# Tokens kept by remainder by four in a hybrid decoder block, and the first head group's values projected per slot

## The chip, the cores and the metric

The kernel runs on one core of one Trainium2 chip. The metric is the device time of one execution in microseconds, taken as the median of several runs. A profile is one more execution, recorded by the hardware profiler, with a time of its own.

## The reference

One layer on 512 tokens of width 1024, all in float32: a half-step SwiGLU network, then a mixing stage of a convolution branch and an attention branch, a second half-step network, a gated per-layer input and a final norm.

```python
h = h + 0.5 * swiglu(rms_norm(h, g_ffn1), ...)          # 1024 -> 2816 -> 1024
u = rms_norm(h, g_mix)
a_glu, q, k, v, gate_logits = split(u @ w_in)
y_conv = conformer_conv(a_glu, ...)                      # GLU, causal depthwise conv of 31, layer norm, swish, matmul
q, k = rotary(q), rotary(k)                              # 12 heads of 128: 3 groups x 4 slots
for (window, dilation) in ((128, 1), (512, 4), (2048, 16)):      # one group each
    o_g, lse_g = dilated_window_attention(q, k, v, dilation, window // dilation)
alpha = softmax over the 3 groups of lse
o = sum_g alpha_g * o_g                                  # per slot; 4 slots x 128
h = h + (sigmoid(gA) * y_conv + sigmoid(gB) * (o @ w_attn_out)) @ w_mix_out
h = h + 0.5 * swiglu(rms_norm(h, g_ffn2), ...)
h = h + sigmoid(rms_norm(h, g_ple) @ w_ple_gate) * (p @ w_ple_proj)
return rms_norm(h, g_final)
```

A query of group 0 sees the 128 tokens before it. In groups 1 and 2 a query sees only tokens at distances that are multiples of 4 (or of 16), so attention there stays within a class of tokens with the same remainder by four.

## The kernel before

Activations are held transposed: a tile has 128 channels on the partitions and the 512 tokens along the free dimension, so 1024 channels are 8 tiles (`KD`). To keep float32 precision each operand is split into a high and a low float32r half, and each product is three matmuls (`mm3`: high by high, high by low, low by high). A `unit` (8 k-steps of `mm3`, 24 matmuls of 512 columns) projects 128 output channels for all tokens.

Weights come in slabs of 128 x 1024, in a fixed list (`slab_order`). `slab(key)` takes the next one and issues the loads of later ones: raw loads six slabs ahead, the remainder for the low half (an ACT copy at L296 and an accumulating DMA at L298) up to four ahead. The POOL queue loads the keys in `POOLED`, SP the others; keys in `RAISED`, such as `v0`, go through one more buffer. Slabs, their halves and two score tiles (`sc`) per slot share 16 buffers (`NW`).

The program is written out in the order in which each engine runs it; nothing is reordered. Work that can wait, above all the convolution's taps on VectorE (L819), lies in the list `bg`; `background(n)` takes n entries from it at places fixed by the constants `N_GLU`, `N_QK`, `N_V0`, `N_V` and `N_GATE`. `soon` holds exponentials and scalings of attention, `between` the subtractions of turned scores, `lns` the layer norm's steps.

The stages around the change:

1. First network. Its last round of `down` adds each of 8 output tiles to the residual h (L703); `into` splits it for the next stage.
2. GLU: 16 units (a gate half and a value half per 128 channels), each product scaled by the inverse norm R, and the taps of the convolution start in `bg`.
3. First values (L1069 to L1080): the values of group 0 for all four slots, 96 matmuls with 128 tokens as the stationary operand and 512 weights moving. The result has tokens on the partitions. The norm factor per token is needed as a column: `rcol` by blocks of 128 tokens, and `rcls` by class, brought by two DMAs through DRAM (`exchange`).
4. Four slots. In each: six units for q and k of the three groups, each followed by `rotary`; then the values of groups 1 and 2 (L1102 to L1111), whose stationary operand is a class of tokens. For slots 1 to 3 and the gates after them, attention of the slot before (`before`) is woven in: `last` makes the scores of groups 1 and 2, `weigh` combines the groups, `turn` transposes the weighted scores, `values` multiplies them. Since the groups' statistics lie by block and by class, `exchange` carries them through DRAM (L885, L886) from one order to the other.
5. 16 units of merge gates with the rest of the convolution, then the attention projection (`pb`), the convolution's (`py`) and the mix (`px`), and the second network.

PSUM has six banks for all of this and two for the convolution's accumulators.

Tokens lie in their natural order. Where an operation needs a class, it reads every fourth token:

```python
def by_class(t):  return t.rearrange("p (i c) -> p c i", c=NB)      # a strided view
def classes(t):   return t.rearrange("p (c i) -> p c i", c=NB)      # 4 contiguous parts
xh, xl = (by_class(z)[:, c] for z in us[4 * j + kk])                # L1107
```

Of the kernel before, what the change touches and what calls it, by code (L numbers as in the profile page):

```python
# [18 lines left out]
P = 128  # L19
# [6 lines left out]
HD = 128  # L26
# [50 lines left out]
N_QK = ((2, 0, 1),) * 2 + ((1, 0, 0),) + ((2, 0, 1),) + ((1, 0, 1),) * 2  # L77
N_V0, N_V = 1, 1
# [52 lines left out]
def block_kernel(ctx: ExitStack, tc: tile.TileContext, a, out):  # L131
# [18 lines left out]

    def bank(n="ps", tag="ps"):
        return psum.tile([P, S], F32, name=name(n), tag=tag, bufs=6 if tag == "ps" else 2)
# [28 lines left out]
    def sources(key):  # L181

        if key[0] == "v0":
            return [(slice(0, 2), slice(i * HD, (i + 1) * HD), blocks_of(a["w_v"][i, key[1]], 2)[:, :, :HD])
                    for i in range(NSLOT)]
# [130 lines left out]
    def split_one():  # L316
        i = state["split"]
        if i in halves:
            state["split"] = i + 1
            return  # L320
        r, q, kind = raws.pop(i), product(order[i]), order[i][0]
        if q is not None:
            w = r.shape[-1]
            h, l = W("wh", F32R)[:, :w], W("wl", F32R)[:, :w]
            spend(0.25 + w * 0.00075, 0.17 + w * 0.001)
            A.activation(h, r, AF.Copy)  # L326
            V.tensor_sub(l, r, h.bitcast(F32))  # L327
            halves[i] = h, l
        elif kind == "pg":
            hs, ls, low = [], [], W("wl", F32R)  # L330
            for c in range(2):
                z = r[:, c * S:(c + 1) * S]
                h, l = T("pgh", F32R), low[:, c * S:(c + 1) * S]
                A.activation(h, z, AF.Copy)
                V.tensor_sub(l, z, h.bitcast(F32))
                hs.append(h)
                ls.append(l)
            halves[i] = (hs, ls)
        else:
            w = r.shape[-1]  # L340
            h, l = W("wh", F32R)[:, :w], W("wl", F32R)[:, :w]
            A.activation(h, r, AF.Copy)
            V.tensor_sub(l, r, h.bitcast(F32))
            halves[i] = (h, l)
        state["split"] = i + 1
# [194 lines left out]
    def ffn(n, xs, norm, resid, after):  # L540
        lo, hi = slice(0, 256), slice(256, 512)
        hid = []
        xn = [None] * 4
# [142 lines left out]
        def down(r, first_, end):  # L686
            ks = ROUNDS[r]
            for m in range(first_, end):
# [14 lines left out]
                V.scalar_tensor_tensor(resid[m], p, 0.5, resid[m], op0=OP.mult, op1=OP.add)  # L703
# [40 lines left out]
    def tables():  # L744
# [19 lines left out]
        do(V.tensor_copy, ang, ip)  # L764
# [38 lines left out]
    for at, w, c in ((0, 2 * P, C_M[0]), (2 * P, P, P), (3 * P, P, C_M[2] - P)):  # L803
        nc.sync.dma_start(mask[:, at:at + w], a["cst"][:, c:c + w])
    conv = {}
    summed = []

    def conv_start(cs, glus):
# [7 lines left out]
        for s in range(1, TAPS):  # L816
            for c, g, acc in zip(cs, glus, accs):
# [4 lines left out]
        def end(c, acc):  # L822
            t = T("cv")
            A.activation(t, acc, AF.Copy)
            conv[c] = t
            if not summed:
                summed.append(T("csum"))
                V.tensor_copy(summed[0], acc)
            else:
                V.tensor_add(summed[0], summed[0], acc)  # L830
        for c, acc in zip(cs, accs):
            bg.append(lambda c=c, acc=acc: end(c, acc))

# [3 lines left out]
    def glu(c, p1, p2, tg, g_, halves_=(0, 1)):  # L837
# [4 lines left out]
        if 1 in halves_:  # L842
            V.tensor_mul(g_, p2, R[0])
            V.tensor_mul(g_, g_, tg)
# [23 lines left out]
    R, rcol = R[0], rcols[0]  # L868
    z = None

    def by_class(t):

        return t.rearrange("p (i c) -> p c i", c=NB)

    def classes(t):
        return t.rearrange("p (c i) -> p c i", c=NB)

    def exchange(what, w, by_block, by_cls):

        for i, (src, dst) in enumerate((by_block, by_cls)):  # L880
# [3 lines left out]
            blk, cls = t.rearrange("(b p) e -> p b e", p=P), t.rearrange("(i c) e -> i c e", c=NB)  # L884
            nc.sync.dma_start((blk, cls)[i], src)  # L885
            nc.sync.dma_start(dst, (cls, blk)[i])  # L886

    rcls = const.tile([P, NB], F32, name="rcls")
    exchange("r", 1, (rcol.rearrange("p (b e) -> p b e", e=1), rcls.rearrange("p (b e) -> p b e", e=1)), (None, None))
# [9 lines left out]
    def rotary(p, n, extra, cls, fill=(lambda: None,) * 2):  # L899
# [14 lines left out]
        if cls:  # L914
            t, hh, ll = by_class(t), classes(h), classes(l)
# [9 lines left out]
    class Attention:  # L925
# [3 lines left out]
        def __init__(self, slot, q, k):  # L929
            self.slot, self.q, self.k = slot, q, k  # L930
# [9 lines left out]
        def score(self, x):  # L940
            p = bank("sc")
            t, lo = self.place(x)
            b = x % NB
            c = slice(b * P, (b + 1) * P)
            if x < NB:
                q, k = self.q[0], self.k[0]
                mm3(p[:, lo:2 * P], q[0][:, c], q[1][:, c], *(z[:, (b - 1) * P + lo:(b + 1) * P] for z in k), True, True)
            else:
                for g in (1, 2):
                    q, k = self.q[g], self.k[g]  # L950
                    mm3(p[:, (g - 1) * P:g * P], q[0][:, c], q[1][:, c], k[0][:, c], k[1][:, c], g == 1, g == 2, True)
            m0 = x // NB * 2 * P
            V.tensor_tensor_reduce(out=t, in0=p[:, lo:2 * P], in1=mask[:, m0 + lo:m0 + 2 * P], op0=OP.add, op1=OP.max,
                                   scale=1.0, scalar=-3.0e38, accum_out=self.own_[:, x, 0:1])

        def scores(self, xs):
            return {i + 4: lambda x=x: self.score(x) for i, x in enumerate(xs)}
# [66 lines left out]
        def values(self, i):  # L1024
# [3 lines left out]
            for j in range(2):  # L1028
                if i < 2:
                    kb = 2 * i + j  # L1030
                    w = P if kb == NB - 1 else 2 * P
                    vh, vl = v0[kb]
                    c, z = slice(self.slot * HD, (self.slot + 1) * HD), slice(j * 2 * P, j * 2 * P + w)
# [8 lines left out]
            if i == 1:  # L1042
                self.first = self.po
            if i == 3:
                t = T("ot")
                A.activation(t.rearrange("p (i c) -> p c i", c=NB), classes(self.po), AF.Copy)
                V.tensor_add(t, t, self.first)
# [20 lines left out]

    pv = [bank("pv") for _ in range(NB)]  # L1069
    for j in range(4):  # L1070
        wh, wl = (blocks_of(z, 2) for z in slab(("v0", j)))
        for b in range(NB):
            for kk in range(2):
                xh, xl = (z[:, b * P:(b + 1) * P] for z in us[2 * j + kk])
                PE.matmul(pv[b], xh, wh[:, kk], start=j == 0 and kk == 0, stop=False)
                PE.matmul(pv[b], xh, wl[:, kk], start=False, stop=False)
                PE.matmul(pv[b], xl, wh[:, kk], start=False, stop=j == 3 and kk == 1)
            background(N_V0)
    v0 = [split(pv[b], "v", rcol[:, b:b + 1]) for b in range(NB)]
    pv = None  # L1080

    before = None
    for s in range(NSLOT):
        q, k = [], []
        n = 0
        now = Attention(s, q, k)
        for g in range(NG):
            for base, dst in ((16, q), (28, k)):
                p = bank("pq")
                unit(p, ("win", base + 4 * g + s), us,  # L1090
                     beside=before.last() if n == 0 and before else now.scores(range(NB)) if n == 3 else {})
                if before is not None:
                    before.step(n)
                if n == 3:
                    now.soft(range(NB))
                dst.append(rotary(p, "qk", N_QK[n], g > 0, *([before.fill(n)] if before else [])))
# [3 lines left out]
                n += 1  # L1100
        q = k = None
        pv = [bank("pv") for _ in range(2)]  # L1102
        for j in range(2):
            wh, wl = (blocks_of(z, 4) for z in slab(("v", s, j)))
            for kk in range(4):
                for c in range(NB):
                    xh, xl = (by_class(z)[:, c] for z in us[4 * j + kk])  # L1107
# [4 lines left out]
                if at == 2 and before is not None:  # L1112
                    before.step(6)
                    before = None
# [191 lines left out]
    def put_out(b):  # L1306
        y = sums.pop(b)
        for i, (t, c, w) in enumerate(done.pop(b)):
# [4 lines left out]
            nc.sync.dma_start(out[b * P:(b + 1) * P, c:c + w], t)  # L1313
# [90 lines left out]
```

## Time and profile before

| | us |
|---|---|
| median of 3 runs (lowest, highest) | 1350.1 (1349.81, 1350.49) |
| the profiled execution | 1348.61 |
| its span | 1346.8 |
| TensorE busy | 1329.9 |
| VectorE busy | 837.3 |
| ScalarE busy | 693.4 |

Lines of the profile's groups read: line, engine, operation, output <- inputs, shape, count, then busy us in all and mean ns of one, then idle time of the engine just before and what ended it. PE is a TensorE matmul, PEld a weight load (it overlaps matmuls), DVE VectorE, ACT ScalarE. Lines of the order of time begin with start and duration in us. Lines of stages read: stretch, its length, busy us (and count) of PE, PEld, DVE, ACT and POOL, the granted TensorE clock, the DMA share and GB/s. Lines of waits read: engine, output, line, `<-` what it waited for, us in all, times, longest. Durations of matmuls overlap; starts do not.

### The profile page before, as it was taken

Reading aid. Unit: us, or ns where it says so; the run is one execution under the profiler, and the core shown is the slowest. Engines: PE = TensorE matmul, PEld = TensorE weight load, DVE = VectorE, ACT = ScalarE, POOL = GpSimd, SP = SyncE. Lnnn points to the kernel's source line nnn. Section 1 sums busy time; section 2 is a strip of 40 time slices with the busy share of each in tenths; the row PEclk is TensorE's granted clock in tenths of the full one; section 3 lists DMA queues with packets and bytes.
Section 4 is the critical chain, followed back from the end, with each engine's and each line's share of the span. In section 5 each row is a group of like instructions: output and inputs, shape, how many; then the busy total and the mean of one; then the engine's idle time right before and its main releaser. Section 6 shows DMA issues by size and latency. Waiting matters only on the chain.

```text
span 1346.8 us, 19358 instructions
## 1 busy us (share of the span) xinstructions
PE 1329.9 (99%) x7490; PEld 1182.7 (88%) x7490; DVE 837.3 (62%) x1371; ACT 693.4 (51%) x981; POOL 225.4 (17%) x294
## 2 busy tenths in 40 slices
PE   9999999999999999999999999999999999999997
PEld 7899899898888889899998888788899899998886
DVE  6985576442469775757665877656784357362465
ACT  6666367464433353636364534334477356555552
POOL 2112011112221231312121220002111111112100
PEclk9999999999999999999999999999999999999999
DMA  9579677878989775848474785233668866869641
GB/s 290 136 168 235 172 157 181 225 168 193 221 196 211 177 154 128 156 102 165 102 166 104 178 205 140 81 105 100 144 167 198 203 174 161 204 159 224 165 94 63
DMA packets 102419, 221.24 MB, mean 164 GB/s; under 512 B 16312, under 2 KB 38200, under 8 KB 102328
## 3 DMA queue, kind: packets, MB, share of 16 engines
q0 software_dynamic: 45856, 133.19, 48.6%
q1 hardware_dynamic: 56184, 86.56, 20.1%
q8 instruction: 59, 0.97, 0.3%
q14 instruction: 32, 0.26, 0.1%
q10 hardware_dynamic: 288, 0.26, 0.1%
HBM read 164.37 MB, written 2.14 MB: 124 GB/s over the span
## 4 chain that ended last, share of the span: by engine, by line
PE 94%; DVE 3%; issue 1%; ACT 1%; DMA 1%; ACTq 0%; SPq 0%; DVEq 0%; POOLq 0%
PE pd L367 8%; PE pd L368 8%; PE pd L369 8%; PE pa L367 6%; PE pa L368 6%; PE pa L369 6%; PE pq L367 3%; PE pq L368 3%; PE pq L369 3%; PE pg L367 3%; PE pg L368 3%; PE pg L369 3%; PE pv L1109 2%; PE pv L1111 2%; PE pv L1110 2%; PE pb L367 1%
## 5 line engine op out<-in xcount | busy, mean ns | idle before, releaser
L298 POOL DMA_DIRECT2D wl<-wr x106 | 91.7, 865 | 528.4 <-ACT wl L296 481.3
L819 DVE SCALAR_TENSOR_TENSOR acc<-glu,taps,acc 128x511 f32<-128x511 f32 (+14 forms) x240 | 161.1, 733 | 0.0
L296 ACT ACTIVATE wl<-wr 128x1024 fp32r<-128x1024 f32 (+1 forms) x106 | 108.1, 1020 | 78.1 <-DMA wl<-wr 34.0
L367 PE MATMUL pd<-hidh,wh 128*128 128x512 f32 x352 | 137.0, 389 | 0.0
L368 PE MATMUL pd<-hidl,wh 128*128 128x512 f32 x352 | 137.0, 389 | 0.0
L369 PE MATMUL pd<-hidh,wl 128*128 128x512 f32 x352 | 136.9, 389 | 0.0
L367 PE MATMUL pa<-bh,wh 128*128 128x256 f32 x432 | 122.5, 283 | 1.6 <-ACT p L666 1.6
L369 PE MATMUL pa<-bh,wl 128*128 128x256 f32 x432 | 122.4, 283 | 0.6 <-DVE wl L327 0.6
L310 ACT ACTIVATE wh<-wr 128x1024 fp32r<-128x1024 f32 (+1 forms) x106 | 107.6, 1015 | 29.8 <-DMA wl<-wr 26.3
L368 PE MATMUL pa<-bl,wh 128*128 128x256 f32 x432 | 122.2, 283 | 0.0
L327 DVE TENSOR_TENSOR wl<-s,wh 128x1024 fp32r<-128x1024 f32 x54 | 66.0, 1223 | 69.5 <-ACT wh L326 69.4
L296 ACT ACTIVATE wl<-wh 128x1024 fp32r<-128x1024 f32 x76 | 79.6, 1050 | 49.1 <-DMA wh<-in_w_in 25.6
L298 POOL DMA_DIRECT2D wl<-in_w_in x56 | 47.9, 855 | 293.6 <-ACT wl L296 279.4
L367 PEld LDWEIGHTS pa<-bh,wh 128*128 128x128 f32 x432 | 82.9, 192 | 2.0 <-ACT p L666 2.0
L369 PEld LDWEIGHTS pa<-bh,wl 128*128 128x128 f32 x432 | 82.9, 192 | 0.8 <-DVE wl L327 0.8
L368 PEld LDWEIGHTS pa<-bl,wh 128*128 128x128 f32 x432 | 82.9, 192 | 0.0
L703 DVE SCALAR_TENSOR_TENSOR gx<-pd,gx 128x512 f32<-128x512 f32 x48 | 32.9, 689 | 79.9 <-PE pd L369 79.9
L367 PE MATMUL pd<-bh,wh 128*128 128x256 f32 x288 | 82.0, 285 | 0.5 <-ACT p L666 0.4
L368 PE MATMUL pd<-bl,wh 128*128 128x256 f32 x288 | 81.5, 283 | 0.0
L369 PE MATMUL pd<-bh,wl 128*128 128x256 f32 x288 | 81.5, 283 | 0.0
L369 PEld LDWEIGHTS pd<-hidh,wl 128*128 128x128 f32 x352 | 66.1, 188 | 13.9
L367 PEld LDWEIGHTS pd<-hidh,wh 128*128 128x128 f32 x352 | 66.1, 188 | 13.5
(293 smaller groups left out, 3767.7 us busy)
## 6 DMA issues: line engine op xcount, KB each, us to landing
wl<-wr POOLq DMA_DIRECT2D x90, 512.0 KB, 5.6
wh<-in_w_in POOLq DMA_DIRECT2D x56, 512.0 KB, 7.1
wl<-in_w_in POOLq DMA_DIRECT2D x56, 512.0 KB, 5.7
wr<-in_w_ffn_up SPq DMA_DIRECT2D x80, 256.0 KB, 4.3
wr<-in_w_ffn_gate SPq DMA_DIRECT2D x78, 256.0 KB, 5.0
wr<-in_w_ffn_down SPq DMA_DIRECT2D x32, 512.0 KB, 5.7
wr<-in_w_ffn_down SPq DMA_DIRECT2D x16, 384.0 KB, 8.3
wl<-wr POOLq DMA_DIRECT2D x16, 384.0 KB, 5.4
```

The costliest lines, as they stand in the source:

```text
L296: A.activation(l.bitcast(F32R), h, AF.Copy, scale=-1.0)
L298: G.dma_start(to, src, accum_op=OP.add)
L310: A.activation(h, r, AF.Copy)
L327: V.tensor_sub(l, r, h.bitcast(F32))
L367: PE.matmul(ps, wh, xh, start=start, stop=False, skip_group_check=part)
L368: PE.matmul(ps, wh, xl, start=False, stop=False, skip_group_check=part)
L369: PE.matmul(ps, wl, xh, start=False, stop=stop, skip_group_check=part)
L703: V.scalar_tensor_tensor(resid[m], p, 0.5, resid[m], op0=OP.mult, op1=OP.add)
L819: bg.append(lambda acc=acc, g=g, w=w, s=s: V.scalar_tensor_tensor(acc[:, s:], g[:, :S - s], w, acc[:, s:], op0=OP.mult, op1=OP.add))
L1109: PE.matmul(po, xh, wh[:, kk], start=at == 0 and c % 2 == 0, stop=False, skip_group_check=True)
L1110: PE.matmul(po, xh, wl[:, kk], start=False, stop=False, skip_group_check=True)
L1111: PE.matmul(po, xl, wh[:, kk], start=False, stop=at == KD - 1, skip_group_check=True)
```

## The change

From the end of the first network on, tokens are kept by class: position c*128 + i holds token 4i + c. The last round of the first network writes h in that order, and the positions, the GLU's output, the convolution's, the mask of group 0 and p are brought into it or out of it where they are made; the convolution itself still runs in natural order. The output rows are written with a step of four. A class is then contiguous. Group 0, which works on blocks of 128 neighbouring tokens, finds its block in four runs of 32 (`by_block`), so its q, k, values and the norm factor for them are read by blocks, and within a block the tokens lie by class too.

The first values' stage goes. Each slot begins with a unit that projects its group 0 values as it does a query (weights stationary, 512 tokens moving), multiplies by R, and transposes the result in four 128 x 128 pieces beside the next unit (`turn0`, at the fifth k-step). `rcls` comes directly from the norm, without DRAM. Two scores share a PSUM bank. An exchange of statistics takes five DMAs instead of two. The sums over the convolution's channels are made from the copies in SBUF.

```diff
-N_QK = ((2, 0, 1),) * 2 + ((1, 0, 0),) + ((2, 0, 1),) + ((1, 0, 1),) * 2
-N_V0, N_V = 1, 1
+N_QK = ((2, 0, 1),) * 6
+N_V0, N_V = 4, 1
+N_TURN = 4
...
-    out += [("v0", j) for j in range(4)]
     for s in range(NSLOT):
+        out += [("v0", s)]
...
+    def by_block(t):
+        return t.rearrange("p (c b i) -> p b c i", c=NB, b=NB)
+    def blocks(t):
+        return t.rearrange("p (b c i) -> p b c i", c=NB, b=NB)
...
-                V.scalar_tensor_tensor(resid[m], p, 0.5, resid[m], op0=OP.mult, op1=OP.add)
+                if n == "1" and r == len(ROUNDS) - 1:
+                    old, resid[m] = resid[m], spare[0]
+                    V.scalar_tensor_tensor(classes(resid[m]), by_class(p), 0.5, by_class(old), op0=OP.mult, op1=OP.add)
+                    spare[0] = old
...
-            V.tensor_mul(g_, p2, R[0])
-            V.tensor_mul(g_, g_, tg)
+            V.tensor_mul(p2, p2, R[0])
+            V.tensor_mul(by_class(g_), classes(p2), classes(tg))
...
-            A.activation(t, acc, AF.Copy)
+            A.activation(classes(t), by_class(acc), AF.Copy)
...
-    R, rcol = R[0], rcols[0]
+    R, rcls = R[0], rcols[0]
...
-            blk, cls = t.rearrange("(b p) e -> p b e", p=P), t.rearrange("(i c) e -> i c e", c=NB)
-            nc.sync.dma_start((blk, cls)[i], src)
-            nc.sync.dma_start(dst, (cls, blk)[i])
-    rcls = const.tile([P, NB], F32, name="rcls")
-    exchange("r", 1, ...)
+            cls = t.rearrange("(c i) e -> i c e", c=NB)
+            blk = t.rearrange("(c b i) e -> c i b e", c=NB, b=NB)
+            if i:
+                nc.sync.dma_start(cls, src)
+            for c in range(NB):
+                z = slice(c * P // NB, (c + 1) * P // NB)
+                if i:
+                    nc.sync.dma_start(dst[z], blk[c])
+                else:
+                    nc.sync.dma_start(blk[c], src[z])
+            if not i:
+                nc.sync.dma_start(dst, cls)
...
-        if cls:
-            t, hh, ll = by_class(t), classes(h), classes(l)
+        if blk:
+            t, hh, ll = by_block(t), blocks(h), blocks(l)
...
             if i == 1:
-                self.first = self.po
+                self.first = T("ot")
+                A.activation(by_block(self.first), blocks(self.po), AF.Copy)
             if i == 3:
-                t = T("ot")
-                A.activation(t.rearrange("p (i c) -> p c i", c=NB), classes(self.po), AF.Copy)
-                V.tensor_add(t, t, self.first)
+                t = self.first
+                V.tensor_add(t, t, self.po)
...
-    pv = [bank("pv") for _ in range(NB)]
-    for j in range(4):
-        wh, wl = (blocks_of(z, 2) for z in slab(("v0", j)))
...
-    v0 = [split(pv[b], "v", rcol[:, b:b + 1]) for b in range(NB)]
...
+        p = bank("pq")
+        unit(p, ("v0", s), us, beside=before.last() if before else {})
+        v0 = T("v0")
+        V.tensor_mul(blocks(v0), by_block(p), by_block(R))
+        if before is not None:
+            before.step(0)
+        some(6)
+        background(N_V0)
+        def turn0():
+            p = bank("pt")
+            for b in range(NB):
+                PE.transpose(p[:, b * P:(b + 1) * P], v0[:, b * P:(b + 1) * P], ident)
+            now.v0 = split(p, "v")
...
                 unit(p, ("win", base + 4 * g + s), us,
-                     beside=before.last() if n == 0 and before else now.scores(range(NB)) if n == 3 else {})
+                     beside=now.scores(range(NB)) if n == 4 else {N_TURN: turn0} if n == 1 else {})
...
-                    xh, xl = (by_class(z)[:, c] for z in us[4 * j + kk])
+                    xh, xl = (classes(z)[:, c] for z in us[4 * j + kk])
...
-                if at == 2 and before is not None:
-                    before.step(6)
...
-            nc.sync.dma_start(out[b * P:(b + 1) * P, c:c + w], t)
+            nc.sync.dma_start(out.rearrange("(i c) e -> c i e", c=NB)[b][:, c:c + w], t)
```

In the new loop n counts from 1 after the values' unit, so `step`, `fill` and `late` act one unit of q or k earlier than before; `step(6)` now follows the sixth q or k unit.

More of the change, by code (lines that the diff above doesn't have):

```diff
@@ L149, in T, with by_class, classes @@
         return act.tile([P, w], dt, name=name(n), tag="t", bufs=NT)
+    def by_class(t):
+        return t.rearrange("p (i c) -> p c i", c=NB)
+    def classes(t):
+        return t.rearrange("p (c i) -> p c i", c=NB)
+    def by_block(t):
+        return t.rearrange("p (c b i) -> p b c i", c=NB, b=NB)
+    def blocks(t):
+        return t.rearrange("p (b c i) -> p b c i", c=NB, b=NB)
     def bank(n="ps", tag="ps"):
@@ L542, in ffn @@
         hid = []
+        spare = []
         xn = [None] * 4
@@ L762, in reduce @@
                 less(t, n, w)
-        do(V.tensor_copy, ang, ip)
+        do(V.tensor_copy, classes(ang), by_class(ip))
         do(V.tensor_scalar, ang, ang, freq, None, op0=OP.mult)
@@ L802, in block_kernel @@
     mask = T("mask")
-    for at, w, c in ((0, 2 * P, C_M[0]), (2 * P, P, P), (3 * P, P, C_M[2] - P)):
+    for at, w, c in ((2 * P, P, P), (3 * P, P, C_M[2] - P)):
         nc.sync.dma_start(mask[:, at:at + w], a["cst"][:, c:c + w])
+    window = T("window")[:, :2 * P]
+    for c in range(NB):
+        nc.sync.dma_start(window[c * P // NB:(c + 1) * P // NB, :],
+                          a["cst"].rearrange("(i c) k -> c i k", c=NB)[c][:, C_M[0]:C_M[0] + 2 * P])
+    bg.append(lambda: V.tensor_copy(mask[:, :2 * P].rearrange("p (z c i) -> p z c i", z=2, c=NB),
+                                    window.rearrange("p (z i c) -> p z c i", z=2, c=NB)))
     conv = {}
@@ L816, in conv_start @@
         for s in range(1, TAPS):
+            if s == 3 and cs[0]:
+                bg.append(lambda: sum_up((cs[0] - 2, cs[0] - 1)))
             for c, g, acc in zip(cs, glus, accs):
@@ L823, in end, with sum_up @@
             t = T("cv")
-            A.activation(t, acc, AF.Copy)
+            A.activation(classes(t), by_class(acc), AF.Copy)
             conv[c] = t
[L826 to L830, printed above, removed]
         for c, acc in zip(cs, accs):
             bg.append(lambda c=c, acc=acc: end(c, acc))
+        if cs[1] == KD - 1:
+            bg.append(lambda: sum_up(cs))
+    def sum_up(cs):
+        if not summed:
+            summed.append(T("csum"))
+            V.tensor_add(summed[0], *(conv[c] for c in cs))
+        else:
+            for c in cs:
+                V.tensor_add(summed[0], summed[0], conv[c])
     R, glus, rcols = [], [], []
@@ L867, in block_kernel, with exchange @@
             glus = []
-    R, rcol = R[0], rcols[0]
+    R, rcls = R[0], rcols[0]
     z = None
[L871 to L880, printed above, removed]
+    def exchange(what, w, by_blk, by_cls):
+        for i, (src, dst) in enumerate((by_blk, by_cls)):
             if src is None:
@@ L938, in place, with score @@
             return self.sc[x // NB][:, x % NB * 2 * P + lo:(x % NB + 1) * 2 * P], lo
[L940 to L954, printed above, removed]
+        def score(self, xs):
+            bank_ = bank("sc")
+            ps = [bank_[:, i * 2 * P:(i + 1) * 2 * P] for i in range(2)]
+            for x, p in zip(xs, ps):
+                b = x % NB
+                c = slice(b * P, (b + 1) * P)
+                if x < NB:
+                    lo, q, k = self.place(x)[1], self.q[0], self.k[0]
+                    mm3(p[:, lo:], q[0][:, c], q[1][:, c], *(z[:, (b - 1) * P + lo:(b + 1) * P] for z in k), True, True)
+                else:
+                    for g in (1, 2):
+                        q, k = self.q[g], self.k[g]
+                        mm3(p[:, (g - 1) * P:g * P], q[0][:, c], q[1][:, c], k[0][:, c], k[1][:, c], g == 1, g == 2, True)
+            for x, p in zip(xs, ps):
+                t, lo = self.place(x)
+                m0 = x // NB * 2 * P
+                V.tensor_tensor_reduce(out=t, in0=p[:, lo:], in1=mask[:, m0 + lo:m0 + 2 * P], op0=OP.add, op1=OP.max,
+                                       scale=1.0, scalar=-3.0e38, accum_out=self.own_[:, x, 0:1])
         def scores(self, xs):
-            return {i + 4: lambda x=x: self.score(x) for i, x in enumerate(xs)}
+            return {i + 4: lambda x=x: self.score((x, x + 1)) for i, x in enumerate(xs) if i % 2 == 0}
         def last(self):
@@ L1084, in block_kernel @@
         q, k = [], []
-        n = 0
-        now = Attention(s, q, k)
+        now = Attention(q, k)
+        p = bank("pq")
+        unit(p, ("v0", s), us, beside=before.last() if before else {})
+        v0 = T("v0")
+        V.tensor_mul(blocks(v0), by_block(p), by_block(R))
+        p = None
+        if before is not None:
[7 more added lines that the diff above has]
+            now.v0 = split(p, "v")
+        n = 1
         for g in range(NG):
@@ L1090, in block_kernel @@
                 unit(p, ("win", base + 4 * g + s), us,
-                     beside=before.last() if n == 0 and before else now.scores(range(NB)) if n == 3 else {})
+                     beside=now.scores(range(NB)) if n == 4 else {N_TURN: turn0} if n == 1 else {})
                 if before is not None:
                     before.step(n)
-                if n == 3:
+                if n == 4:
                     now.soft(range(NB))
-                dst.append(rotary(p, "qk", N_QK[n], g > 0, *([before.fill(n)] if before else [])))
+                dst.append(rotary(p, "qk", N_QK[n - 1], g == 0, *([before.fill(n)] if before else [])))
                 p = None
```

35 lines of the change are left out of this document (17 added, 18 removed).

## The prediction

> **What bounds the kernel now.** I read the page first, then what TensorE waits for, then its groups by form.
>
> ```profile
> span 1346.8 us, 19358 instructions
> PE 1329.9 (99%) x7490; PEld 1182.7 (88%) x7490; DVE 837.3 (62%) x1371; ACT 693.4 (51%) x981; POOL 225.4 (17%) x294
> PE 94%; DVE 3%; issue 1%; ACT 1%; DMA 1%; ACTq 0%; SPq 0%; DVEq 0%; POOLq 0%
> PE py L368 <- DVE cvl L385: 2.4, 2, 1.3
> ```
>
> TensorE is busy for all but 16.9 us, and the last line heads the list of what it waits for: 2.4 us in all, in 2 times. (Its granted clock is the 1.00 in the stage rows below.) So time can come only from fewer or faster TensorE instructions, and time is lost only where the others newly let it wait. VectorE (62%) and ScalarE (51%) have room on average. The next question is whether every matmul runs as fast as its shape allows.
>
> ```profile
> L1109 PE MATMUL pv<-wh,xsh 128*128 128x256 f32 x128 | 50.9, 397 | 0.0
> L367 PE MATMUL pa<-bh,wh 128*128 128x256 f32 x432 | 122.5, 283 | 1.6 <-ACT p L666 1.6
> L1109 PEld LDWEIGHTS pv<-wh,xsh 128*128 128x128 f32 x128 | 42.0, 328 | 0.0
> L367 PEld LDWEIGHTS pa<-bh,wh 128*128 128x128 f32 x432 | 82.9, 192 | 2.0 <-ACT p L666 2.0
> L1075 PEld LDWEIGHTS pv<-wh,xsh 128*128 128x128 f32 x32 | 6.0, 188 | 1.3
> 563.92 0.40 PE L1109 MATMUL pv<-wh,xsh 128*128 128x256 f32 x1
> ...
> 571.38 0.40 PE L1111 MATMUL pv<-wh,xsl 128*128 128x256 f32 x1
> ```
>
> ```profile
> 235.28 0.28 PE L369 MATMUL pd<-bh,wl 128*128 128x256 f32 x1
> ...
> 237.08 0.28 PE L369 MATMUL pd<-bh,wl 128*128 128x256 f32 x1
> ```
>
> They do not. The values of groups 1 and 2 (L1109 to L1111, three lines of 128) have 256 moving columns, as the mixed products of the networks have. Durations overlap, so I take starts: from 563.92 to 571.38 there are 32 steps, 0.233 us each; from 235.28 to 237.08 there are 15, 0.120 us each. The same 256 columns cost nearly double. What differs is the weight load: 328 ns against 192. Its source is `by_class(z)[:, c]`, every fourth token, 16 bytes apart; L1075 loads from the same tiles, contiguous, in 188. This part is bound by the strided load.
>
> **The change, part by part.**
>
> *The strided load goes.* With tokens kept by remainder, `classes(z)[:, c]` is 128 neighbours. 96 matmuls per slot in 4 slots, 384 x (0.233 - 0.120) = 43.4 us, all of it on TensorE and so on the path. Bounds: no gain, if the layout is not what sets the 0.233 (a rival below), and 46.8 if it fell to the 0.111 of a 128-column step (the row of transposes below shows 0.90 us for 8). I take 0.120, the row with the same columns.
>
> The Trainium skill, "SBUF — State Buffer" (the cacheline note under "Door 1: The DMA port swizzle"), states 16-byte lines, with a penalty where each access crosses to a new one; fp32 at a step of four is that case, and the 328 against 188 ns agrees.
>
> *The first group's values.* Before, 96 matmuls of 512 columns in a stage of their own; after, 24 per slot, still 512 columns, weights and tokens changing places. Same number, same pace: 0. New are four transposes per slot.
>
> ```profile
> 562.48 0.90 PE pt L1016 x8
> 444.90:466.80 21.90, 21.90 (x98) 18.16 (x97) 17.63 (x27) 5.63 (x7) 5.85 (x9) 1.00 0.95 207
> 523.60:588.70 65.10, 65.10 (x329) 59.22 (x328) 43.38 (x84) 34.58 (x64) 15.29 (x20) 1.00 0.63 130
> ```
>
> 16 x 0.90/8 = +1.8 us. They come after four k-steps, 12 matmuls of 21.90/98 = 0.22 us, 2.7 us after the unit's end, and need only VectorE's product with R, at most 1.1 us by the strided rows below. Pairing scores changes neither their number nor columns: 0.
>
> *VectorE in a slot.* The second row above is slot 1: 65.1 us, VectorE 43.4. After: 65.1 + 5.4 (24 x 0.223) + 0.5 (transposes) - 10.9 = 60.1 us. VectorE gains 8 convolution taps (N_QK sums to 18 against 14, N_V0 gives 4), the product with R and the low half of the turned values, and loses strided reads.
>
> ```profile
> L819 DVE SCALAR_TENSOR_TENSOR acc<-glu,taps,acc 128x511 f32<-128x511 f32 (+14 forms) x240 | 161.1, 733 | 0.0
> 541.22 0.69 DVE L920 TENSOR_TENSOR qkl<-rot,qkh 128x512 fp32r<-128x512 f32 x1
> 554.21 1.11 DVE L920 TENSOR_TENSOR qkl<-rot,qkh 128x512 fp32r<-128x512 f32 x1 [0.55 <-ACT qkh L916]
> L1046 ACT ACTIVATE ot<-po 128x512 f32<-128x512 f32 x4 | 4.3, 1084 | 14.6 <-PE po L369 14.6
> ```
>
> L920 takes 0.69 on a contiguous `rot` (group 0) and 1.11 by class. Four of six per slot were strided; after, only group 0's two are, by blocks, in runs of 32. No row shows runs of 32, so between 0.69 and 1.11. Sum: 43.4 + 8 x 0.73 + 1.1 + 0.7 - 4 x 0.42 + (0 to 0.8) = 49.3 to 50.1 of 60.1 us. It stays under TensorE by 10 us, which is the cover for all of this. If the cover fails in a single unit, the units behind it (5.4 us each) absorb it, since PSUM has six banks.
>
> *Strided writes and reads elsewhere.* The first network's last round writes h by class (8 operations), the GLU writes by class (8), ScalarE copies 8 convolutions by class, and the positions, the window mask and pT once each. Each is priced between 0 and +0.42 us on VectorE, with two strided inputs perhaps double; on ScalarE less than the 1.08 us that its whole strided copy (L1046) takes. The tightest places:
>
> ```profile
> 403.00:414.00 11.00, 11.00 (x50) 9.12 (x49) 9.96 (x16) 2.65 (x3) 1.41 (x2) 1.00 1.05 267
> 356.81 0.69 DVE L703 SCALAR_TENSOR_TENSOR gx<-pd,gx 128x512 f32<-128x512 f32 x1 [1.25 <-PE pd L369]
> 358.29 0.75 DVE L388 SCALAR_TENSOR_TENSOR xsl<-gx,xsh 128x512 fp32r<-128x512 f32 x1 [0.79 <-ACT xsh L387]
> ```
>
> In the GLU, VectorE is busy 9.96 of 11.0 us; +0.42 per pair of units fits. At the end of the first network the chain after the last matmul is 356.81 to 359.04, 2.2 us; the next unit's eighth k-step comes 21 x 0.22 = 4.7 us after it, so +0.8 is hidden. Where ScalarE empties an accumulator, the next pair's first tap waits up to two such copies, 2.2 us, but the two sums that stood there (1.5 us by the row below) move behind it. Cost: 0.
>
> *The end of the convolution.* 128 list entries are spent in the slots against 112 before (with the first values' stage), so 60 entries remain for the gates against 72 (four entries of sums are added, the 12 GLU calls take 72 in both): 10 gate units instead of 12.
>
> ```profile
> 795.87 1.48 DVE L830 TENSOR_TENSOR csum<-csum,acc 128x512 f32<-128x512 f32 x2
> 834.54 2.47 DVE cv L1144 x4
> 843.59 0.50 PE py L368
> ```
>
> The sums now end about 796, VectorE's normalizing runs until `py` starts, and that is the 2.4 us wait quoted first. Two gate units (four steps of the list `lns`) earlier, it ends inside the attention projection. -2.4 us, bounds 0 and -2.4.
>
> *DMAs and queues.* SP no longer moves R through DRAM. It carries four loads for each first-values slab, now amid the slots, and five transfers instead of two per exchange of statistics, 0.33 us of issue each.
>
> ```profile
> 601.77 0.33 SPq L885 DMA_DIRECT2D st<-own  x1
> 603.18 0.37 SPq L886 DMA_DIRECT2D other<-st  x1
> 625.04 0.37 SPq L885 DMA_DIRECT2D st<-own  x1
> 633.86 0.33 SPq L886 DMA_DIRECT2D other<-st  x1
> other<-st SPq DMA_DIRECT2D x8, 4.0 KB, 3.4
> ```
>
> ```profile
> 607.59 0.69 DVE L901 TENSOR_TENSOR rot<-pq,nl 128x512 f32<-128x512 f32 x1 [0.68 <-PE pq L369]
> 608.20 0.16 DVE L987 TENSOR_TENSOR jm<-own,other 128x8 f32<-128x8 f32 x1
> 612.23 1.10 DVE L920 TENSOR_TENSOR qkl<-rot,qkh 128x512 fp32r<-128x512 f32 x1 [0.40 <-ACT qkh L916]
> ```
>
> The exchange that the next slot's L987 needs is the first pair: issued 601.77, read 603.18, used 608.20. It moves one unit earlier with its users, the exponentials now directly behind the values' unit; three more reads add 1.1 us of issue. Cost 0, bound below. The slab loads behind it on SP are issued six slabs ahead. POOL issues the same slabs as before.
>
> **Sum.** -43.4 + 1.8 - 2.4 = -44.0 us. The profiled execution took 1348.61 us (span 1346.8 and 1.8 around it), so 1304.6. The median of the runs, 1350.1, is 1.5 above it: 1306 us.
>
> **The rivals.**
>
> *Late statistics (up to 1324).* The k unit of group 0 now carries the weighing (L987) in its rotary, and its scores come at the fifth k-step two units on. The rotary with the weighing runs 5.7 us in the last fence (607.59 to 613.33); with two taps more (+1.4) and no stride (-0.4) it takes 6.7, while TensorE needs 36 x 0.223 = 8.0 to get there: 1.3 us of slack. From the write's issue to L987 there are now 6.4 us (601.77 to 608.20). If the write took as long as in the second pair (8.8 us, 625.04 to 633.86), with 1.5 us of issue and 3.4 to land, 13.7 would be needed: 7.3 late, 6.0 beyond the slack, in three slots, +18. For: the DMA share rises, 9 slabs in 60.1 us instead of 8 in 65.1, from 0.63 to about 0.77. Against: 603.18 followed its write by 1.4 us, and L987 did not wait.
>
> *The weights cannot be fed (slower, 1362).* Attention takes 444.9 to 718.8, 273.9 us, for 36 slabs. It must do it in about 230, 6.4 us a slab. Place: the two value slabs, which TensorE will use up in 11.5 us instead of 22.4, and the first values' slab, which needs three W buffers of the sixteen. It turns slower when a slab takes over 7.6 us (273.9/36); at 8.0 it would be 288, +14 less the 2.4 won later.
>
> ```profile
> 359.40:444.90 85.50, 85.50 (x383) 70.89 (x382) 63.90 (x114) 28.42 (x33) 20.18 (x28) 1.00 0.86 196
> wh<-in_w_in POOLq DMA_DIRECT2D x56, 512.0 KB, 7.1
> wh<-in_w_v POOLq DMA_DIRECT2D x16, 256.0 KB, 5.6
> ```
>
> Against: the GLU used 16 slabs in 85.5 us, 5.3 each, without a wait of TensorE; landing takes 5.6 to 7.1 us, with four to six slabs in flight.
>
> *The layout is not the limit (1349.5).* Then the pace of L1109 stays 0.233, and only +1.8 - 2.4 remain. For: nothing in the rows but that slow matmuls and slow loads coincide. Against: L1075, same tiles, 188 ns.
>
> The Trainium skill, "TensorE: Matmul & The Clock Gate" ("LDWEIGHTS (loading the stationary operand)"), gives a load's time by its columns alone, P/1.2, and so would leave L1109 as slow as it is; the trace disagrees, with 328 and 188 ns for the same 128 columns.
>
> **How the numbers follow.** The sum holds, with small waits at most: 0.75, 1303 to 1310. Late statistics, in part or whole, or another wait of a few us per slot: 0.17, 1310 to 1324. Layout not the limit: 0.04. Not fed: 0.04, of which 0.03 is slower than before. Predicted 1306; low end 1302, by the 0.111 step; high end 1320, into the late statistics, which leaves out about 0.15 in all. A measurement of this kernel tells about 0.2% (2.7 us) from no change. Faster: 0.75 + 0.17 + 0.01 = 0.93; same 0.04; slower 0.03.
>
> **What would show it.** Right: weight loads of the group 1 and 2 values at about 190 ns and starts 0.12 us apart; no wait of `py`; slots near 60 us; the stage before them gone. Late statistics would show as a wait of `sc` for VectorE; hunger for weights as waits of `pv` or `pq` for a DMA, ScalarE or POOL. Wrong would be TensorE idle inside the slots by more than 5 us in all, or loads still near 330 ns.

## The result, and the profile after

| us | before | after |
|---|---|---|
| median (lowest, highest) | 1349.95 (1348.64, 1350.49) | 1309.11 (1308.09, 1310.11), 4 runs |
| profiled execution, its span | 1348.61, 1346.8 | 1310.11, 1308.3 |

The ratio of the times is 0.9699, 95% interval 0.9682 to 0.9716: 40.8 us less. Forecast were 1306, in a range of 1302 to 1320.

The page of the kernel after, its totals:

```profile
span 1308.3 us, 19429 instructions
PE 1289.5 (99%) x7506; PEld 1140.9 (87%) x7506; DVE 836.6 (64%) x1375; ACT 683.9 (52%) x981; POOL 225.1 (17%) x294
```

TensorE still is the bound. It has 16 instructions more (the transposes) and 40.4 us less work, of 38.5 us less span. So its idle time did not shrink (16.9 us before, 18.8 now): what was won is work. The groups by form, and starts of the values' matmuls:

```profile
L1158 PE MATMUL pv<-wh,xsh 128*128 128x256 f32 x128 | 36.4, 284 | 0.0
L1158 PEld LDWEIGHTS pv<-wh,xsh 128*128 128x128 f32 x128 | 24.3, 189 | 0.0
```

```profile
490.72 0.28 PE L1158 MATMUL pv<-wh,xsh 128*128 128x256 f32 x1
...
493.96 0.28 PE L1158 MATMUL pv<-wh,xsh 128*128 128x256 f32 x1
```

The same 128 loads take 189 ns instead of 328, and 27 steps from 490.72 to 493.96 are 0.120 us each instead of 0.233. That is the forecast pace.

What TensorE waits for, in the places that the change touched:

```profile
PE sc L390 <- DVE qkl L962: 0.7, 1, 0.7
PE pp L1305 <- ACT wh L365: 0.7, 1, 0.7
PE pg L389 <- DVE sg L1236: 0.5, 1, 0.5
PE pp L1307 <- DVE wl L366: 0.5, 1, 0.5
```

The wait of `py`, 2.4 us before, is gone; these four small ones are new (and 0.2 us of `hT` at the very end). The windows of the whole attention (from the first unit of the slots' part to the first gate), of slots 1 and 2, and of the `py` stage (the next fence has that stage before the change):

```profile
446.74:679.45 232.71, 231.97 (x1347) 204.41 (x1346) 185.15 (x353) 125.26 (x233) 64.94 (x86) 1.00 0.80 161
498.30:558.40 60.10, 60.10 (x357) 53.16 (x356) 45.85 (x92) 35.35 (x68) 17.50 (x23) 1.00 0.79 157
558.40:619.40 61.00, 60.26 (x357) 53.20 (x356) 47.23 (x95) 33.52 (x64) 16.11 (x21) 1.00 0.78 157
801.14:844.66 43.52, 43.52 (x193) 36.05 (x192) 24.95 (x31) 11.08 (x14) 0.00 (x0) 1.00 0.30 97
```

```profile
839.17:885.80 46.63, 44.25 (x194) 35.81 (x192) 31.70 (x42) 19.02 (x26) 0.00 (x0) 1.00 0.28 90
```

By the first starts of TensorE in each stage, the span's 38.5 us go like this:

| stage | before | after | difference |
|---|---|---|---|
| up to the attention | 445.08 | 446.74 | +1.66 |
| attention (first values and slots) | 273.34 | 232.71 | -40.63 |
| gates and attention projection, up to `py` | 120.75 | 121.69 | +0.94 |
| `py` | 46.63 | 43.52 | -3.11 |
| end of the second network, up to `pp` | 54.43 | 55.28 | +0.85 |
| `pp` | 6.83 | 7.74 | +0.91 |
| the rest | | | +0.9 |

The first row is not the change's: in a second profile of the same kernel (the first experiment) the attention begins at 445.37. The others come back there, to 0.3 us.

### The profile page after: what moved, and what is told of

Its sections match the earlier page's. It is cut to its first block, busy times and chain, and to the rows that moved or that the text cites. A ratio compares the mean times of both kernels' runs of the same rounds, so it can differ in the third digit from the quotient of the medians.

```text
span 1308.3 us, 19429 instructions
## 1 busy us (share of the span) xinstructions
PE 1289.5 (99%) x7506; PEld 1140.9 (87%) x7506; DVE 836.6 (64%) x1375; ACT 683.9 (52%) x981; POOL 225.1 (17%) x294
## 4 chain that ended last, share of the span: by engine, by line
PE 86%; DMA 5%; DVE 4%; ACT 2%; issue 2%; SPq 0%; DVEq 0%; ACTq 0%; POOLq 0%
PE pd L389 8%; PE pd L391 8%; PE pd L390 8%; PE pa L389 6%; PE pa L390 6%; PE pa L391 6%; PE pq L389 3%; PE pq L391 3%; PE pq L390 3%; PE pg L389 2%; PE pg L390 2%; PE pg L391 2%; DMA wl<-wr 2%; PE pb L391 2%; PE pb L389 2%
## 5 line engine op out<-in xcount | busy, mean ns | idle before, releaser
L389 PE MATMUL pq<-xsh,wh 128*128 128x512 f32 x224 | 88.7, 396 | 0.0
L391 PE MATMUL pq<-xsh,wl 128*128 128x512 f32 x224 | 87.3, 390 | 0.0
L390 PE MATMUL pq<-xsl,wh 128*128 128x512 f32 x224 | 87.3, 390 | 0.0
```

Of the source, the lines that this page charges most:

```text
L389: PE.matmul(ps, wh, xh, start=start, stop=False, skip_group_check=part)
L390: PE.matmul(ps, wh, xl, start=False, stop=False, skip_group_check=part)
L391: PE.matmul(ps, wl, xh, start=False, stop=stop, skip_group_check=part)
```

## The experiments

The time of the kernel before was 1349.27 us in experiments 1, 2, 5 and 6, which ran together, and 1349.28 in the others. The theory: the contiguous weight load alone brings some 43 us, the rest of the change costs a few, at two places of its own. The rival: the rest (first values as queries, other order) is itself a part of the gain, or the costs are scatter between executions.

**1. The kernel after once more**, no edit.

> The changed kernel once more, beside the next three on one chip, as their measure. Theory and rivals alike: 1308 to 1310 us, with the wait of the weighing (L1033) for its transfer near 12.6 us in all, the loss of about 0.9 us each in one slot and in the gates, and the two waits of the ple projection (pp), 0.7 and 0.5 us. If instead these losses are scatter of one execution, they lie elsewhere or are gone here.

1309.11 us (1308.63 to 1309.61); ratio 0.9702, interval 0.9689 to 0.9715. Its waits of TensorE, and VectorE's wait for the other groups' statistics in slots and gates:

```profile
PE sc L390 <- DVE qkl L962: 0.9, 2, 0.7
PE pp L1305 <- ACT wh L365: 0.7, 1, 0.7
PE pp L1307 <- DVE wl L366: 0.5, 1, 0.5
PE pg L389 <- DVE sg L1236: 0.5, 1, 0.5
```

```profile
DVE jm L1033 <- DMA other<-st: 14.8, 4, 7.3
```

The four waits are there again, to a tenth or two: they belong to the kernel. Behind two of them stands a DMA, which the kernel before never waited for at that line (its L987).

**2. The contiguous load alone**, in the kernel before. The values are then those of other tokens; nothing else changes.

```diff
-                    xh, xl = (by_class(z)[:, c] for z in us[4 * j + kk])
+                    xh, xl = (classes(z)[:, c] for z in us[4 * j + kk])
```

> The kernel before with one edit: the stationary operand of the values of groups 1 and 2 is 128 neighbouring tokens instead of every fourth (so these values belong to other tokens; token order, first values' stage and everything else stay). Theory, the strided weight load sets the pace: loads near 190 ns instead of 328, starts 0.120 us apart instead of 0.233, 384 x 0.113 = 43.4 us less, 1306 to 1307. Rival, the layout is not the limit: 1350, with starts still 0.233 apart. Second rival, the weights cannot be fed faster: loads of 190 ns but waits of pv for DMA or ScalarE, and a time between.

1305.47 us (1305.27 to 1305.71); ratio 0.9674, interval 0.9661 to 0.9687.

```profile
L1109 PEld LDWEIGHTS pv<-wh,xsh 128*128 128x128 f32 x128 | 24.5, 192 | 0.0
PE py L368 <- DVE cvl L385: 2.4, 2, 1.3
```

One edit of a line brings 43.8 us, and the wait of `py` stays. The whole change brings 40.2 (1349.27 to 1309.11). So the rest of it, which includes the 3.1 us won at `py`, costs 3.6 net.

**3. The stride put back**, in the kernel after (again other tokens' values).

```diff
-                    xh, xl = (classes(z)[:, c] for z in us[4 * j + kk])
+                    xh, xl = (by_class(z)[:, c] for z in us[4 * j + kk])
```

> The kernel after, with one thing changed: the stationary operand of group 1 and 2's values is read with a step of four again (by_class at L1156; the rows of the product then belong to other tokens than the slot's scores). Everything else of the change stays: tokens by class, first values as queries, 16 transposes, ten gate units for the sums. Theory (the strided load is worth 43.8 us wherever it stands, and the rest of the change costs some 4): 1309.1 + 43.8 = 1352.9, loads near 328 ns, steps of 0.233 us. Rival (part of the after kernel's gain is due to the layout of other operands, or the stride is hidden better by the slots as they are now): below 1349, that is less than +40; then the rest of the change is not a loss.

1352.72 us, one run: 43.6 more than after. The term adds the same in both kernels, and without it the change would have made the kernel 3.4 us slower. The rival, that the other parts earn some of the gain, falls.

**4. Which steps are slow**: the kernel before, its weight load with another step for each k-step (other tokens' values for three of them).

```diff
-                    xh, xl = (by_class(z)[:, c] for z in us[4 * j + kk])
+                    step = (4, 2, 3, 1)[kk]
+                    xh, xl = (z[:, c:c + (P - 1) * step + 1:step] for z in us[4 * j + kk])
```

> The kernel before, in which the weight load of L1109 has a step of 4, 2, 3 and 1 float32 (16, 8, 12 and 4 bytes) for kk = 0, 1, 2 and 3, on lines of their own (the values are then those of other tokens). 96 of the 384 matmuls have each step. Theory (the Trainium skill, 'SBUF - State Buffer', Cachelines: two hits on a 16-byte line give full speed): step 2 loads as step 1, near 190 ns and 0.12 us a matmul; step 4 near 328 and 0.233; step 3, which has a line of its own for two of four elements or more, between, nearer to step 4. Time 1349.3 - 2 x 10.9 - (0 to 5) = 1322 to 1328. Rival (any step over one makes the load slow): steps 2, 3 and 4 all near 328, time 1349.3 - 10.9 = 1338. Third (the load's time grows with the step): about 190, 235, 280, 328, time 1349.3 - 10.9 x (1 + 0.67 + 0.33) = 1327.5, told from the first by the rows of steps 2 and 3, not by the time.

1321.65 us, one run, just under the 1322 that was the low end of what was expected. The loads by line, in the order of steps 4, 2, 3 and 1:

```profile
L1111 PEld LDWEIGHTS pv<-wh,xsh 128*128 128x128 f32 x32 | 10.4, 324 | 0.0
L1115 PEld LDWEIGHTS pv<-wh,xsh 128*128 128x128 f32 x32 | 6.4, 200 | 0.0
L1119 PEld LDWEIGHTS pv<-wh,xsh 128*128 128x128 f32 x32 | 8.3, 260 | 0.0
L1123 PEld LDWEIGHTS pv<-wh,xsh 128*128 128x128 f32 x32 | 6.1, 190 | 0.0
```

Step 2 is almost free (200 ns against 190), step 3 lies between (260), step 4 is slow (324). So it is not "any stride", and not growth in proportion either, which would have 235 for step 2. The matmuls follow: their starts lie 0.120 us apart at steps 1 and 2, 0.176 at step 3 and 0.235 at step 4. From step 1 to 2 the load grows by 10 ns, from there by 60 and 64 a step. Counted in stretches of 16 bytes, 128 elements touch 32, 64, 96 and 128 of them, so a floor and then about 2 ns for each stretch more would fit, and so would a floor and then a price for the distance itself. Steps above 4 would tell the two apart; they were not run. The Trainium skill, "SBUF — State Buffer" ("Door 1: The DMA port swizzle", the note on cachelines), asks for two hits on each 16-byte line: by that step 2 is free and step 4 is not, and the rows agree. The same note would let fp32 stride by four for free; the rows of 324 and 260 ns do not agree with that.

**5. The exchange's scratch in token order**, in the kernel after. This is the order that it had before; a partition of the write by class then holds 32 neighbouring bytes instead of four pieces of 8.

```diff
-            cls = t.rearrange("(c i) e -> i c e", c=NB)
-            blk = t.rearrange("(c b i) e -> c i b e", c=NB, b=NB)
+            cls = t.rearrange("(i c) e -> i c e", c=NB)
+            blk = t.rearrange("(b i c) e -> c i b e", c=NB, b=NB)
```

> The changed kernel with another order of the scratch in DRAM through which the statistics are exchanged: token order (4 classes of a place side by side) instead of class order, so that the write by class is 32 bytes in one piece per partition as before the change, instead of four pieces of 8 bytes. Theory, the late statistics come from the pieces: the single write lands in about 1.4 us instead of 4.6 to 5.0, L1033 waits under 4 us in all instead of 12.6, the losses in the slot and in the gates go, 1 to 2 us less than the changed kernel: 1307 to 1308. Rival, the rings are fuller (DMA share 0.78 instead of 0.63): landing stays at about 5 us, the wait near 12 us, time as the changed kernel.

1306.84 us (1306.38 to 1308.08); ratio 0.9686, interval 0.9672 to 0.9699: 2.3 us less than after. The queue of SP in slot 2 (the write by class, then the four reads of it), first after, then this kernel:

```profile
569.71 0.38 SPq L923 DMA_DIRECT2D st<-own  x1
574.72 1.97 SPq L927 DMA_DIRECT2D other<-st  x4
```

```profile
568.70 0.34 SPq L923 DMA_DIRECT2D st<-own  x1
570.18 1.79 SPq L927 DMA_DIRECT2D other<-st  x4
```

The reads are issued when the write has landed: 5.0 us after its issue in the one, 1.5 in the other. With it the waits of `sc` and `pg` are gone, and VectorE's wait at L1033 falls to 5.4 us (2 times, longest 4.0; under 4 in all was expected), all of it covered. Slot 2 up to its values falls from 49.42 to 48.47 us, as long as slot 3 was (48.48), and the gates with the projection from 121.69 to 120.75.

The experiment shows that the order in DRAM makes the write late. It does not show that the length of the pieces does, because the edit also moved them: pieces that lay 8 bytes apart now lie 32 apart. The other half of each exchange, four writes by block, is in pieces of 8 bytes in both orders, and it too became faster. Issues with their size and median time to landing, after (two rows), then here:

```profile
st<-own SPq DMA_DIRECT2D x16, 1.0 KB, 5.3
st<-own SPq DMA_DIRECT2D x4, 4.0 KB, 4.8
```

```profile
st<-own SPq DMA_DIRECT2D x16, 1.0 KB, 2.7
st<-own SPq DMA_DIRECT2D x4, 4.0 KB, 1.4
```

So 8-byte pieces that lie side by side may be what is slow. Length and spacing were not separated.

**6. pT split in its own order**, in the kernel after; the stationary operand of its product then has a step of four.

```diff
-            if kind == "pT":
-                r = r.rearrange("p (k i c) -> p k c i", k=2, c=NB)
-                h, l = (z.rearrange("p (k c i) -> p k c i", k=2, c=NB) for z in (h, l))
...
-                z = slice(kk * S + b * P, kk * S + (b + 1) * P)
-                PE.matmul(p, pTh[:, z], wh[:, kk], start=kk == 0, stop=False)
+                xh, xl = (by_class(z[:, kk * S:(kk + 1) * S])[:, b] for z in (pTh, pTl))
+                PE.matmul(p, xh, wh[:, kk], start=kk == 0, stop=False)
```

> The changed kernel with pT split in its natural order (contiguous on ScalarE and VectorE) and instead every fourth token taken by the weight load of the ple projection (L1305 to L1307, 48 matmuls of 512 columns). Theory: a strided load costs 0.233 us per matmul whatever the columns are, so beside 512 columns (0.227) it costs 48 x 0.006 = 0.3 us, and the split's strided 2.0 us on each engine, which made pp wait 0.7 and 0.5 and drew 1.8 us, is gone: 1.5 us less, 1307.5. Rival: the longer load adds its 0.14 us to every matmul: 48 x 0.14 = 6.7 us more, less 1.8: 1314.

1307.6 us (1307.4 to 1307.85); ratio 0.969, interval 0.9677 to 0.9703: 1.5 us less than after. Its loads by form, and its matmuls in order of time:

```profile
L1303 PEld LDWEIGHTS pp<-wh,wl 128*128 128x128 f32 x16 | 5.0, 311 | 0.0
```

```profile
1236.41 0.40 PE L1302 MATMUL pp<-wh,wh 128*128 128x512 f32 x1
...
1237.12 0.39 PE L1302 MATMUL pp<-wh,wh 128*128 128x512 f32 x1
```

No wait of `pp` is left. The load takes 311 ns, yet the matmuls, of 512 columns, start 0.236 us apart (three steps in 0.71): 0.009 more than the 0.227 of contiguous ones. So the same stride that costs 0.113 us a matmul beside 256 columns is almost hidden beside 512.

**7. The taps of the convolution placed as before**, in the kernel after: fewer in the slots, more left for the gates.

```diff
-N_QK = ((2, 0, 1),) * 6
+N_QK = ((2, 0, 1),) * 2 + ((1, 0, 0),) + ((2, 0, 1),) + ((1, 0, 1),) * 2
```

> The kernel after, with N_QK as it was before (14 entries of the list per slot instead of 18), so that 76 entries are left for the gates instead of 60: at six per unit that is 13 gate units instead of 10 (12 before). Theory (the wait of py fell because the convolution's sums end two gate units earlier): py waits for VectorE's cvl again, 2.4 us or more, the projection's stage goes from 43.5 back to 46 to 49, and the slots are no faster, since VectorE was no limit there: 1311 to 1315. Rival (the wait went for another reason, such as the sums being taken from SBUF): no wait of py, 1309. Second rival (the taps in the slots are what makes sc wait for qkl): then slot 2's 0.9 us come back, and the sum is 1309 + 2.4 - 0.9 or less.

1321.04 us (1319.98 to 1323.12); ratio 0.9794, interval 0.9777 to 0.981. The direction is the theory's, the size is not: +11.9 us, where I expected 2 to 6.

```profile
PE py L389 <- ACT cvh L406: 2.9, 1, 2.9
PE py L390 <- DVE cvl L407: 1.7, 3, 1.3
PE sc L390 <- DVE qkl L962: 1.1, 1, 1.1
```

The last sums over channels, after (first row) and here:

```profile
748.13 1.49 DVE L875 TENSOR_TENSOR csum<-csum,cv 128x512 f32<-128x512 f32 x2
```

```profile
763.29 1.49 DVE L875 TENSOR_TENSOR csum<-csum,cv 128x512 f32<-128x512 f32 x2 [0.55 <-ACT cv L862]
```

They end 85.7 us after the first gate (764.8 less 679.10) instead of 70.2 (749.6 less 679.45). Before, it was 78.9 (797.35 less 718.42). Gates with projection and the `py` stage together take 175.5 us here, 10.3 more than after and 8.1 more than before; attention takes 1.0 more than after. Not all of the 8.1 is late sums. In the gates the attention woven in holds TensorE up for 2.0 us, which it did not before. And behind the 2.9 us wait of `py` the granted clock of TensorE falls to about half, 0.53 in this row:

```profile
805.60:812.00 6.40, 5.09 (x12) 3.65 (x13) 5.74 (x10) 6.24 (x10) 0.00 (x0) 0.53 0.00 0
```

From 807.70 to 811.68 nine steps of TensorE take 3.98 us, where nine at 0.227 take 2.04. Behind the two waits of `py` in the kernel before, 1.0 and 1.3 us long, the clock stayed at 1.00. That leaves about 4 us for sums that end 6.8 us later: a late sum costs up to its delay, and a wait that grows long costs the clock on top. My expectation took the 2.4 us of twelve gate units as the price of thirteen, and had no term for the clock or for attention. The wait of `sc` stays with fewer taps, so they were not its cause.

**8. Both mends**, experiments 5 and 6 in one kernel.

> The kernel after, with both of the edits that won alone: the exchange's scratch in token order (1306.84, so -2.3) and pT split in its own order with the strided stationary operand (1307.6, so -1.5). The two places are 600 us apart and share no buffer. Theory (the change lost time at these two places, each for itself): the gains add, 1309.1 - 2.3 - 1.5 = 1305.3, range 1304.5 to 1306.3; no wait of sc or pg for VectorE and none of pp; weight loads of L1302 to L1304 near 311 ns. Rival (what one edit wins is partly taken back at the end, since the tail waits for ACT's table load and for the last loads whatever comes before): 1306 to 1307, as the first edit alone. It would then be no faster than the kernel before with the contiguous load alone (1305.5); by the theory it equals it.

1305.79 us (1305.66 to 1307.91); ratio 0.9681, interval 0.9666 to 0.9695. The gains add, to half a us (1305.3 was expected). The time alone hardly tells this from the rival, which had 1306 to 1307; the waits do. In its profile TensorE waits for nothing in slots, gates or `pp`; VectorE's wait at the weighing is down to this:

```profile
DVE jm L1030 <- DMA other<-st: 2.6, 1, 2.6
```

This version beats both kernels, and it stands where the contiguous load alone stood (1305.47): the sums' earlier end (3.1 us at `py`) pays for the transposes (attention is 1.8 us longer) and for some 1.3 us at `pp` and behind it.

## Why the prediction was right, point by point

**The strided load, -43.4: right.** Measured -43.8 alone and -43.6 in reverse, by the pace that the prediction took from the networks' row with the same columns, 0.120 us. The bound of 0.111 was not reached. The rival "the layout is not the limit" is excluded by experiment 2, where nothing but the layout changed.

**The transposes, +1.8: right.** In the kernel after, four of them together take 0.44 us:

```profile
455.07 0.44 PE pt L1131 x4
```

**Slots of 60.1 us: right** for slot 1, with 60.10 in the window; slot 2, which waited, took 61.00. The rival "the weights cannot be fed" did not come: the DMA share rose to 0.79, as forecast (0.77), and no `pv` or `pq` waited.

**VectorE in a slot, 49.3 to 50.1 us: too high.** It was 45.9 and 47.2. The reads by blocks, in runs of 32, were priced at 0 to 0.8 and cost nothing: all of them stand in one group at the contiguous price (the first row below). In slot 1 the eight more taps added 5.0 us of busy time instead of 5.8, and the product with R took 0.69 instead of 1.1. Two sums over channels, 1.4 us, stood in that slot before and do not now, which the sum left out. The last 0.8 us are not explained.

```profile
L962 DVE TENSOR_TENSOR qkl<-rot,qkh 128x512 fp32r<-128x512 f32 x24 | 16.6, 692 | 1.9 <-ACT qkh L958 0.7
L887 DVE TENSOR_TENSOR glu<-pa,gg 128x512 f32<-128x512 f32 x8 | 8.6, 1069 | 1.3 <-ACT gg L883 0.6
L730 DVE SCALAR_TENSOR_TENSOR gx<-pd,gx 128x512 f32<-128x512 f32 x7 | 7.4, 1060 | 7.3 <-PE pd L391 7.3
```

The GLU's write by class, in the second row, has one strided operand and costs 1.07. The first network's last round, in the third, has two strided inputs and costs 1.06, no more than one; "perhaps double" was too much. ScalarE's copy of a convolution, bounded by 1.08, takes 0.60 where it reads PSUM by class, against 0.59 before.

**"Strided writes and reads elsewhere ... Cost: 0": failed at pT.** It is split once, but just ahead of its use, with nothing between. ScalarE and VectorE, one after the other:

```profile
1230.57 2.04 ACT L365 ACTIVATE wh<-wr 128x1024 fp32r<-128x1024 f32 x1
```

```profile
1232.63 1.98 DVE L366 TENSOR_TENSOR wl<-wr,wh 128x1024 fp32r<-128x1024 f32 x1 [1.11 <-ACT wh L365]
```

The same two take 1.04 and 1.22 us contiguous. 1.8 us more stood on the path; the stages `pp` and the one ahead of it lost 0.85 and 0.91, and experiment 6 got 1.5 back. The prediction named the two tightest places and did not look at the third. At the other strided places no new wait of TensorE appeared.

**The end of the convolution, -2.4: right in kind, -3.1 in size.** The bound of 2.4 was too low, though no other wait stood in that stage. The profile counts a wait from the end of the matmul before it, 0.39 us after its start, while the next one follows after 0.23 where nothing waits; and the first matmul behind a wait is followed only after 0.34. By starts, the two waits before cost 2.9 of the 3.1 us. Kernel before:

```profile
839.17 0.39 PE L367 MATMUL py<-cvh,wh 128*128 128x512 f32 x1
840.59 0.50 PE L368 MATMUL py<-cvl,wh 128*128 128x512 f32 x1 [1.03 <-DVE cvl L385]
```

Experiment 7 shows that the time of the sums decides whether `py` waits.

**DMAs and queues, "Cost 0, bound below": mis-sized.** The prediction let the write of the statistics land in 1.4 us as before; it took 5.0 (experiment 5). The cause lay in the diff: scratch in class order cuts the write by class into pieces of 8 bytes. The trace before held a hint. The "second pair" that the prediction quotes, 625.04 and 633.86, is a write by block, and that one was in pieces of 8 bytes, side by side, already then: it was read back after 5.0, 8.9, 8.8 and 7.0 us, the write by class, in pieces of 32 bytes, after 1.4 each time. But the slow ones ran at DMA shares of 0.32 to 0.67 and the fast ones at 0.05, so that trace alone could not tell the layout from the rings. The rival "late statistics" had the right place and the wrong mechanism, fuller rings. Here is the write in the gates, where the DMA share is 0.05, and who waits for it:

```profile
692.62 0.38 SPq L923 DMA_DIRECT2D st<-own  x1
697.26 1.98 SPq L927 DMA_DIRECT2D other<-st  x4
```

```profile
692.60:697.20 4.60, 4.60 (x22) 3.79 (x21) 4.53 (x8) 3.81 (x4) 1.89 (x3) 1.00 0.05 1
```

```profile
706.76 0.17 DVE L1033 TENSOR_TENSOR jm<-own,other 128x8 f32<-128x8 f32 x1 [7.35 <-DMA other<-st]
```

That is 4.6 us at the share at which the old layout took 1.4, so fuller rings are not the cause. The price stayed small for the reason the rival gave: 1.3 us of slack and the units behind. Of VectorE's 14.8 us of waiting (experiment 1), TensorE felt 1.9: 0.95 in slot 2 and 0.94 in the gates (experiment 5).

**The sum.** -44.0 was forecast, against 40.2 to 40.8 measured. Late statistics (2.3), pT (1.5) and 0.7 behind `pp` are the difference, less 0.7 at `py` and 0.4 at the load. So the mechanism was right and two terms set to nothing were not; that the time still came out within the first branch (1303 to 1310) is luck to the extent of about 1 us, by which two terms were better than forecast. Of the 0.7 at the end, 0.4 lie where the sigmoid's table load now stands behind a wait for `pg`. That was not tried.

```profile
1261.60 1.28 ACT L1334 ACT_TABLE_LOAD   x1 [4.29 <-PE pg L1321]
```

## What to carry to other kernels

Compare weight loads of the same shape by their duration: a slower one points to its layout, and it costs only where the moving columns are too few to cover it (0.113 us a matmul at 256, 0.009 at 512). When a layout is turned, follow it to the places where something is used right after it is made, and into DRAM, where the order of the pieces can make a small transfer land 3 us later. Work moved into a stage where its engine has slack wins nothing in that stage; what it wins stands in the stage that it left, once the cover there is used up.

## What the runs showed of the hardware that was not expected

- A 128-column float32r weight load takes 190, 200, 260 and 324 ns at steps of 1, 2, 3 and 4 elements (experiment 4), 311 where the moving operand has 512 columns (step 4, experiment 6).
- A write of 4 KB to DRAM in 8-byte pieces that lie side by side was read back after 4.4 to 5.5 us in the kernel after and 5.0 to 8.9 in the one before; in 32-byte pieces after 1.4 to 1.6 (before and experiment 5), seen only at DMA shares up to 0.10. At a share of 0.05 it was 4.6 against 1.5.
- On VectorE runs of 32 neighbouring float32 cost as much as a contiguous row (0.69 us for 512), while a step of four costs 1.06 to 1.11, with one strided operand or with two. A ScalarE copy that writes SBUF with a step of four took 1.08 us (L1046 before), one that reads PSUM with that step 0.60.
- After a wait of TensorE of 2.9 us its granted clock was 0.53 for the next 6.4 us (experiment 7); after waits of 1.0 and 1.3 us it stayed at 1.00.
